# First tile and first weights asked for by two queues, and norm weights spread in eight single passes

## The chip, the cores and the metric

The kernel runs on one core of a Trainium2 chip. The metric is device time in microseconds of one execution; the median of several runs counts. Times inside the profile are microseconds from the start of the span.

## The reference

One layer of a gated streaming encoder on x of 1024 tokens by 1024 features, float32. Every row is normalised, projected once, and the columns of the projection feed two branches.

```python
h = rmsnorm(x, norm_g[l])
proj = h @ w_in[l]
q, k, v, za, u, vs, zs, gm = jnp.split(proj, IN_SPLITS, axis=-1)
a = window_sink_attention(rope(q), rope(k), v, att_sinks[l])
a = (a * jax.nn.silu(za)) @ w_att_out[l]
sgo = chunked_spatial_gating(gelu(u), gelu(vs), sg_w[l], sg_b[l], sg_ln_g[l], sg_ln_b[l])
sgo = (sgo * jax.nn.silu(zs)) @ w_sg_out[l]
ga, gs = jnp.split(jax.nn.sigmoid(gm + b_merge[l]), 2, axis=-1)
x = x + (ga * a + gs * sgo) @ w_o[l]
return rmsnorm(x, final_g)
```

with `rmsnorm(x, g) = x * rsqrt(mean(x*x) + EPS) * g`.

## The kernel before

Matrix products are made at float32 accuracy from single-pass fp32r operands: each operand is split into a high part, which is a cast to fp32r on ScalarE (ACT), and a low part, which is the difference, on VectorE (DVE) or GpSimd (POOL). A product is then three matmuls: high by high, high by low, low by high. Most of the kernel works in such products on two-by-two blocks with seven block products (`gemm_pair`); that part isn't touched by the diff.

The diff lies in the head, the first 20 us or so. The rows of x come in as eight tiles of 128 tokens (`load_x`), tile 0 as two halves of 512 columns. `scale_of` squares a tile and sums it on ACT, and `rstd_of` makes the reciprocal root: a square root on ACT (L145) and four small operations on DVE. `normed_tile` then, for each half of the columns, multiplies the tile by that root and by the norm weights on DVE (L625), transposes it in four 128x128 steps on TensorE (L632), casts the result to the high part on ACT (L635) and subtracts for the low part on DVE (L636).

The norm weights must lie on all 128 partitions for L625. They come in as two rows of 512 on partitions 0 and 32 of a zeroed tile `g_rows` (load at L563), and two fp32 matmuls with a selector `of_g` of ones and zeros spread them into the PSUM tiles `g_in` (L575). Matmuls on a tile of ones, whose result isn't used (`keep_busy`, L568), run ahead of the spread (six) and behind it (two), and `after` fixes this order.

The first columns of the big product are those of the spatial gate's input (`vs`). Its weights come in eight tiles of 512 KB; of the first four, numbers 0 and 1 go to `T_t3h`, 2 and 3 to `T_t4h` (`load_vs`, L655), number 0 in two halves. `split_vs` splits number 0 by halves, with its casts on ACT (L672) and its subtractions on POOL (L675), the others whole (L662 on ACT, L664 on DVE). `vs_gemm(0)` (L685) is the first product; the others are L646.

All of the head's loads are issued by SP, in the order tile 0 (two halves), norm weights, weights 0 (two halves), weights 1, row tile 1, weights 2, weights 3, row tile 2, row tile 3. A scheduler puts the instructions of each engine in order; each engine then works through its own list and waits on semaphores.

Of the kernel before, what the change touches and what calls it, by code (L numbers as in the profile page):

```python
# [25 lines left out]
F32 = mybir.dt.float32  # L26
F32R = mybir.dt.float32r
BF16 = mybir.dt.bfloat16
AF = mybir.ActivationFunctionType
# [3 lines left out]
P = 128  # L33
D = 1024
S = 1024
KC = D // P
HALF = 512
# [8 lines left out]
W_VS = 34  # L46
# [8 lines left out]
def hybrid_tile(  # L55
# [16 lines left out]
    nc = tc.nc  # L72
# [8 lines left out]
    def nm(s):  # L81
        count[0] += 1
        return f"{s}_{count[0]}"

    def bank(tag, dt=F32):
        return psum.tile([P, 512], dt, name=nm("ps_" + tag), tag="ps_" + tag, bufs=2)

    def mtile(shape, dt, tag, bufs, pool=None):
        return (pool or main).tile(shape, dt, name=nm(tag), tag=tag, bufs=bufs)
# [4 lines left out]
    def raw_tile():  # L94
        return mtile([P, D], F32, "wr", 3)
# [4 lines left out]

    eps_sb = const.tile([P, 1], F32, name="eps_sb")
    nc.gpsimd.memset(eps_sb[:], EPS)
    ones_b = mtile([P, HALF], BF16, "T_b22l", 1)
    nc.vector.memset(ones_b[:], 1.0)
    g_rows = mtile([P, D], F32, "wh", 3)[:, 0:HALF]
    nc.vector.memset(g_rows, 0.0)
    of_g = mtile([P, D], F32, "wl", 3)[:, 0 : 2 * P].rearrange("p (j m) -> p j m", j=2)
    nc.gpsimd.memset(of_g, 0.0)
    for j in range(2):
        nc.gpsimd.memset(of_g[32 * j : 32 * j + 32, j, :], 1.0)  # L110
    ident = const.tile([P, P], F32, name="ident")
    make_identity(nc, ident[:])
    warm = const.tile([P, 1], F32, name="warm")
    nc.scalar.activation(warm[:], eps_sb[:], AF.Sqrt)

    sink_sb = const.tile([P, 8], F32, name="sink_sb")
    nsink_sb = const.tile([P, 8], F32, name="nsink_sb")
# [59 lines left out]
    def after(second, first):  # L177

        tc.add_manual_dep(
            second.ins,  # L180
            first.ins.name,
            mybir.DependencyInfo(mybir.DependencyClass.NoSync, mybir.DependencyReason.DATA),
            reason="order",
        )
# [5 lines left out]
    def slot(name, shape=(P, 4, HALF), dt=F32R):  # L190

        return mtile(list(shape), dt, "T_" + name, 1)
# [362 lines left out]
    def load_x(t, parts=1):  # L555
        xt = raw_tile()
        for c in range(parts):
            cs = slice(c * D // parts, (c + 1) * D // parts)
            nc.sync.dma_start(xt[:, cs], x[t * P : (t + 1) * P, cs])
        return xt  # L560

    x_in = {0: load_x(0, 2)}
    nc.sync.dma_start(g_rows[0:33:32, :], norm_g.rearrange("(j n) -> j n", j=2))  # L563
    junk = mtile([P, D], F32, "wl", 3)

    def keep_busy(n):
        return [
            nc.tensor.matmul(idle[:], ones_b[:, 0:P], ones_b[:], start=True, stop=True) for _ in range(n)  # L568
        ]

    idle = bank("o")
    g_in = [bank("sc") for _ in range(2)]
    behind = keep_busy(6)[-1]
    for j in range(2):
        spread = nc.tensor.matmul(g_in[j][:], of_g[:, j, :], g_rows, start=True, stop=True)  # L575
        after(spread, behind)
        behind = spread
    after(keep_busy(2)[0], behind)

    hb = new_b(("b11", "b21"))  # L580

# [18 lines left out]
    def scale_of(t):  # L600
        xt = x_in[t] if t in x_in else load_x(t)
        if t == 0:
            s0, s1, base, half_base = (stat() for _ in range(4))
            for c, ss in enumerate((s0, s1)):
                nc.scalar.activation(junk[:, half_of(c)], xt[:, half_of(c)], AF.Square, accum_out=ss[:])
            nc.vector.tensor_scalar(base[:], s0[:], 1.0 / D, EPS, op0=ALU.mult, op1=ALU.add)
            nc.vector.tensor_scalar_mul(half_base[:], base[:], -0.5)
            return xt, rstd_of(s1[:], 1.0 / D, (base[:], half_base[:]))
        ss = stat()
        square = nc.scalar.activation(junk[:], xt[:], AF.Square, accum_out=ss[:])  # L610
        if t == 1:

            after(square, casts[-1])
        return xt, rstd_of(ss[:], 1.0 / D)

    def normed_tile(t, scale=None):
        xt, r = scale or scale_of(t)
        if t == 4:
            hb.update(new_b(("b22",)))
            f.update((n, slot(at, dt=F32)) for n, at in (("f12", "t4h"), ("f22", "t3h")))  # L620
        turned = []
        for j in range(2):
            cs = half_of(j)
            scalings.append(
                nc.vector.scalar_tensor_tensor(  # L625
                    xt[:, cs], xt[:, cs], r[:], g_in[j][:], op0=ALU.mult, op1=ALU.mult
                )
            )
            pt = bank("o" if t == 1 else "tp")
            for i in range(4):  # L630
                k = j * 4 + i
                nc.tensor.transpose(pt[:, i * P : (i + 1) * P], xt[:, k * P : (k + 1) * P], ident[:])  # L632
            p3 = pt[:].rearrange("p (k c) -> p k c", k=4)
            hi, lo = quarter_of(t, j)
            casts.append(nc.scalar.copy(hi, p3))  # L635
            los.append(nc.vector.tensor_sub(lo, p3, hi.bitcast(F32)))  # L636
            turned.append((f[f"f{j + 1}{t // 4 + 1}"][:, :, tokens(t)], p3))
            if t:
                nc.scalar.copy(*turned.pop())
        return turned  # L640
# [7 lines left out]

    vs_w, vs_casts = [], []

    def load_vs(c):
        parts = 2 if c == 0 else 1
        for i in range(parts):
            cs = slice(i * D // parts, (i + 1) * D // parts)
            nc.sync.dma_start(vs_raw[c // 2][:, c % 2, cs], w[W_VS + c][:, cs])  # L655

    def split_vs(c):

        raw = vs_raw[c // 2][:, c % 2, :].rearrange("p (k n) -> p k n", k=2)
        hi, lo = (v[c // 2][:, 2 * (c % 2) : 2 * (c % 2) + 2, :] for v in vs_split)  # L660
        if c:
            cast = nc.scalar.copy(hi, raw)  # L662
            vs_casts.append(cast)
            sub = nc.vector.tensor_sub(lo, raw, hi.bitcast(F32))  # L664
            if c == 1:
                after(sub, los[1])
            elif c == 2:
                after(cast, roots[1])
                after(sub, scalings[3])
        else:  # L670
            for k in range(2):
                cast = nc.scalar.copy(hi[:, k, :], raw[:, k, :])  # L672
                if k == 0:
                    after(cast, roots[0])
                nc.gpsimd.tensor_tensor(lo[:, k, :], raw[:, k, :], hi[:, k, :].bitcast(F32), op=ALU.subtract)  # L675
        vs_w.extend((hi[:, k, :], lo[:, k, :]) for k in range(2))
# [11 lines left out]
        nc.scalar.copy(xh[:, t, 0:HALF], acc[:])  # L688

    unsplit = normed_tile(0)  # L690
    vs_raw = [slot(n, (P, 2, D), F32) for n in ("t3h", "t4h")]
    vs_split = [[slot(n + e) for n in ("t1", "t2")] for e in "hl"]
    load_vs(0)
    load_vs(1)
    split_vs(0)
    x_in[1] = load_x(1)
    split_vs(1)
    second = scale_of(1)
    for c in (2, 3):
        load_vs(c)  # L700
    x_in[2] = load_x(2)
    normed_tile(1, second)
    for c in (2, 3):
        split_vs(c)
# [71 lines left out]
    for c in range(4):  # L776
        if c + 2 < 4:
            weights.append(vs_weights(c + 2))
        for t in range(NT):
            wh, wl = weights[c]  # L780
# [696 lines left out]
    with tc.manual_schedule(engines={mybir.EngineType.PE, mybir.EngineType.Activation, mybir.EngineType.DVE}):  # L1477
        p = 0
# [292 lines left out]
    for p in range(4):  # L1771
        n, t, acc, x11 = N_PAIRS + p, T_ORDER[p], accs[p], firsts[p]
# [203 lines left out]
```

## Time and profile before

| | us |
|---|---|
| median of 3 runs | 921.29 |
| lowest and highest run | 920.75, 921.34 |
| the profiled execution | 921.45 |
| its span | 919.7 |
| TensorE busy | 907.4 |
| ACT busy | 529.6 |
| DVE busy | 691.2 |

In a row of the timeline the first number is the start, the second the time that the row's instructions took together, then engine, line, operation, output and inputs, how many there were, and in brackets how long the engine had been idle before and what ended that. SPq and ACTq are the queues' DMA issues. In the chain of waits a row is start, length, and what held the end up then. In the table of windows the columns are the stretch and its length, busy time of TensorE, its weight loads, DVE, ACT and POOL with the number of instructions, the granted clock, the share of DMA time and GB/s.

### The profile page before, as it was taken

The numbers are of one execution on the slowest core, as the hardware profiler recorded it, in microseconds if no ns is written. First come the engines' busy times: TensorE is split into PE (matmuls) and PEld (weight loads), VectorE is DVE, ScalarE is ACT, GpSimd is POOL, SyncE is SP. The second block draws the span as 40 slices with busy tenths as digits, with TensorE's granted clock in tenths as the row PEclk, the third lists the DMA queues.
The fourth block names the chain that finished last, engine by engine and source line by source line (L and its number), as shares of the span: only waits on it lengthen the run. The fifth ranks groups of instructions, "written<-read, shape, count | busy, mean of one in ns | idle before, by whom it ended". The sixth has DMA issues, their size and how long they took to land.

```text
span 919.7 us, 13199 instructions
## 1 busy us (share of the span) xinstructions
PE 907.4 (99%) x4296; PEld 749.4 (81%) x4296; DVE 691.2 (75%) x1233; ACT 529.6 (58%) x1058; POOL 141.9 (15%) x213
## 2 busy tenths in 40 slices
PE   8999999999999999999999999999999999999996
PEld 5888888888888888888888888888888888887885
DVE  6774776656678678777887788765599689579986
ACT  7942433334445456877778878444476475467443
POOL 1002222213011001222111110001110111210012
PEclk9999999999999999999999999999999999999999
DMA  7328788877788879999999994775568666998633
GB/s 241 122 97 217 172 150 185 177 186 212 242 270 260 270 249 328 266 241 260 255 344 246 266 246 144 284 252 179 173 204 304 226 206 179 282 322 271 206 115 114
DMA packets 129024, 206.10 MB, mean 224 GB/s; under 512 B 12634, under 2 KB 59738, under 8 KB 128956
## 3 DMA queue, kind: packets, MB, share of 16 engines
q1 hardware_dynamic: 107292, 146.27, 49.3%
q0 software_dynamic: 21376, 58.73, 27.2%
q8 instruction: 34, 0.56, 0.3%
q14 instruction: 34, 0.28, 0.1%
q10 hardware_dynamic: 288, 0.26, 0.1%
HBM read 148.46 MB, written 90.31 MB: 260 GB/s over the span
## 4 chain that ended last, share of the span: by engine, by line
PE 88%; DVE 4%; ACT 3%; DMA 3%; issue 1%; SPq 0%; ACTq 0%
PE ps_mm L388 40%; PE ps_o L388 24%; PE ps_mm L646 6%; PE ps_tp L388 4%; PE ps_sc L1196 2%; PE ps_o L1320 2%; PE ps_sc L388 2%; PE ps_tp L857 2%; PE ps_tp L646 1%; PE ps_sc L646 1%; PE ps_o L646 1%; PE ps_tp L1267 1%; ACT pr L1231 1%; PE ps_tp L1272 1%; ACT pr L1254 1%
## 5 line engine op out<-in xcount | busy, mean ns | idle before, releaser
L174 ACT CAST wh<-s 128x1024 fp32r<-128x1024 f32 (+1 forms) x78 | 77.9, 1002 | 78.9 <-PE ps_mm L388 25.4
L175 DVE TENSOR_TENSOR wl<-s,wh 128x1024 fp32r<-128x1024 f32 (+1 forms) x78 | 90.9, 1166 | 21.6 <-ACT wh L174 21.4
L175 DVE TENSOR_TENSOR wl<-wr,wh 128x1024 fp32r<-128x1024 f32 (+1 forms) x64 | 60.3, 944 | 53.0 <-ACT wh L174 53.0
L174 ACT CAST wh<-wr 128x1024 fp32r<-128x1024 f32 (+1 forms) x64 | 53.0, 829 | 77.2 <-PE ps_mm L388 33.7
L1231 ACT ACTIVATE pr<-ps_sc,sm 128x192 f32<-128x192 f32 (+2 forms) x128 | 51.2, 407 | 30.6 <-DVE sm L1222 22.0
L333 POOL DMA_DIRECT2D sums<-in_w_dram x48 | 36.6, 861 | 207.4 <-PE ps_mm L388 86.4
L388 PE MATMUL ps_o<-T_b22h,wh 128*128 128x512 f32 x148 | 59.3, 401 | 0.0
L388 PE MATMUL ps_o<-T_t1h,wl 128*128 128x512 f32 x148 | 58.0, 392 | 0.4 <-DVE wl L175 0.4
L388 PE MATMUL ps_o<-T_t1h,wh 128*128 128x512 f32 x148 | 58.3, 394 | 0.0
L388 PE MATMUL ps_o<-T_b22l,wh 128*128 128x512 f32 x148 | 57.8, 390 | 0.0
L388 PE MATMUL ps_o<-T_b22h,wl 128*128 128x512 f32 x148 | 57.7, 390 | 0.0
L388 PE MATMUL ps_o<-T_t1l,wh 128*128 128x512 f32 x148 | 57.7, 390 | 0.0
L388 PE MATMUL ps_mm<-T_t4h,wh 128*128 128x512 f32 (+1 forms) x144 | 55.8, 388 | 0.0
L388 PE MATMUL ps_mm<-T_t2h,wh 128*128 128x512 f32 x140 | 55.5, 396 | 0.0
L388 PE MATMUL ps_mm<-T_t4l,wh 128*128 128x512 f32 (+1 forms) x144 | 55.3, 384 | 0.0
L388 PE MATMUL ps_mm<-T_t4h,wl 128*128 128x512 f32 (+1 forms) x144 | 55.3, 384 | 0.0
L388 PE MATMUL ps_mm<-T_b11h,wh 128*128 128x512 f32 x140 | 55.2, 394 | 0.0
L388 PE MATMUL ps_mm<-T_t3h,wh 128*128 128x512 f32 x140 | 54.8, 391 | 0.0
L388 PE MATMUL ps_mm<-T_b11l,wh 128*128 128x512 f32 x140 | 54.7, 391 | 0.0
L388 PE MATMUL ps_mm<-T_b11h,wl 128*128 128x512 f32 x140 | 54.6, 390 | 0.0
L388 PE MATMUL ps_mm<-T_t3h,wl 128*128 128x512 f32 x140 | 54.6, 390 | 0.0
L388 PE MATMUL ps_mm<-T_t2h,wl 128*128 128x512 f32 x140 | 54.5, 390 | 0.0
(405 smaller groups left out, 2470.2 us busy)
## 6 DMA issues: line engine op xcount, KB each, us to landing
wr<-in_w_dram SPq DMA_DIRECT2D x80, 256.0 KB
sums<-in_w_dram POOLq DMA_DIRECT2D x24, 512.0 KB, 6.7
s<-sums SPq DMA_DIRECT2D x24, 512.0 KB
wr<-in_w_dram SPq DMA_DIRECT2D x16, 512.0 KB
q_hl<-qhl SPq DMA_DIRECT2D x16, 512.0 KB
q<-q_hl SPq DMA_DIRECT2D x64, 128.0 KB
y_dr<-x POOLq DMA_DIRECT2D x28, 256.0 KB, 6.5
sums<-in_w_dram POOLq DMA_DIRECT2D x24, 256.0 KB, 7.4
```

What stands on the lines that cost most here:

```text
L174: nc.scalar.copy(hi, src)
L175: return nc.vector.tensor_sub(lo, src, hi.bitcast(F32))
L333: return lambda: paced(nc.gpsimd.dma_start(dst, src, accum_op=op))
L388: mm = nc.tensor.matmul(acc, lt, rt, start=fresh and k == 0 and n == 0, stop=k == 3 and n == 2, skip_group_check=True,)
L646: mm = nc.tensor.matmul(acc, lt, rt, start=k == 0 and n == 0, stop=k == KC - 1 and n == 2)
L857: nc.tensor.matmul(pm[:, t * P : (t + 1) * P], xh[:, half * 4 + t, g * P : (g + 1) * P], bias[-1][1][:, g % 4, :], start=True, stop=True,)
L1196: nc.tensor.matmul(sc[:, i, lo:hi], q_of[:, c, i * P : (i + 1) * P], kt[:, f, lo:hi], start=f == 0, stop=f == 1,)
L1231: nc.scalar.activation(st.pr[:, i, place_of(c, lo, hi)], st.sc[c][:, i, lo:hi], AF.Exp, bias=st.nmax[:, c, i : i + 1], scale=-1.0, accum_o ...
L1254: nc.scalar.mul(v, v, st.inv[:, c, i : i + 1])
L1267: nc.tensor.transpose(st.inner[0:wide, at : at + P], st.pr[:, i, place_of(c, 64 if st.t else P, 192)], ident[:])
L1272: nc.tensor.transpose(st.ends[0:wide, i * P : (i + 1) * P], st.pr[:, i, P : P + wide], ident[:])
L1320: nc.tensor.matmul(st.po[:, cs], lt, rt, start=i == 0, stop=i == len(terms) - 1, skip_group_check=True)
```

## The change

The second half of row tile 0 and the second half of weights 0 are issued by ACT's queue instead of SP's, ahead of ACT's table load, and the loads of weights 0 are issued right behind the norm weights. The norm weights come in as four rows of 256 on partitions 0, 32, 64 and 96. DVE casts them to a high part and subtracts for a low part, and eight fp32r matmuls of 256 columns (four rows by two parts) take the place of the two fp32 matmuls of 512. The selector has four blocks instead of two and is cast on DVE. Four keep-busy matmuls follow the spread instead of two. The splitting of weights 3 gets the same two order constraints as that of weights 2.

In the resulting order of instructions ACT casts the second half of weights 0 ahead of the square root of tile 0, where it was behind it, and casts weights 3 ahead of a copy of tile 0's transposes; SP issues the load of row tile 4 behind four small loads and that of `sg_w` instead of ahead of them. Everything else keeps its order on every engine.

```diff
+    g_rows = mtile([P, D], F32, "wh", 3)[:, 0:256]
+    nc.vector.memset(g_rows, 0.0)
     ones_b = mtile([P, HALF], BF16, "T_b22l", 1)
     nc.vector.memset(ones_b[:], 1.0)
-    g_rows = mtile([P, D], F32, "wh", 3)[:, 0:HALF]
-    nc.vector.memset(g_rows, 0.0)
-    of_g = mtile([P, D], F32, "wl", 3)[:, 0 : 2 * P].rearrange("p (j m) -> p j m", j=2)
-    nc.gpsimd.memset(of_g, 0.0)
-    for j in range(2):
-        nc.gpsimd.memset(of_g[32 * j : 32 * j + 32, j, :], 1.0)
+    rows_of = mtile([P, D], F32, "wl", 3)[:, 0:HALF]
+    nc.gpsimd.memset(rows_of, 0.0)
+    for j in range(4):
+        nc.gpsimd.memset(rows_of[32 * j : 32 * j + 32, j * P : (j + 1) * P], 1.0)
+    of_g = mtile([P, D], F32R, "wl", 3)[:, 0:HALF]
+    nc.vector.tensor_copy(of_g, rows_of)
+    g_split = mtile([P, D], F32R, "wh", 3)
+    g_parts = [g_split[:, i * 256 : (i + 1) * 256] for i in range(2)]
...
-    nc.scalar.activation(warm[:], eps_sb[:], AF.Sqrt)
...
-            nc.sync.dma_start(xt[:, cs], x[t * P : (t + 1) * P, cs])
+            (nc.scalar if c else nc.sync).dma_start(xt[:, cs], x[t * P : (t + 1) * P, cs])
         return xt
 
+    def load_vs(c):
+        parts = 2 if c == 0 else 1
+        for i in range(parts):
+            cs = slice(i * D // parts, (i + 1) * D // parts)
+            (nc.scalar if i else nc.sync).dma_start(vs_raw[c // 2][:, c % 2, cs], w[W_VS + c][:, cs])
+
     x_in = {0: load_x(0, 2)}
-    nc.sync.dma_start(g_rows[0:33:32, :], norm_g.rearrange("(j n) -> j n", j=2))
+    nc.sync.dma_start(g_rows[0:97:32, :], norm_g.rearrange("(j n) -> j n", j=4))
+    vs_raw = [slot(n, (P, 2, D), F32) for n in ("t3h", "t4h")]
+    load_vs(0)
+    nc.scalar.activation(warm[:], eps_sb[:], AF.Sqrt)
+    nc.vector.tensor_copy(g_parts[0], g_rows)
+    nc.vector.tensor_sub(g_parts[1], g_rows, g_parts[0].bitcast(F32))
...
     behind = keep_busy(6)[-1]
-    for j in range(2):
-        spread = nc.tensor.matmul(g_in[j][:], of_g[:, j, :], g_rows, start=True, stop=True)
-        after(spread, behind)
-        behind = spread
-    after(keep_busy(2)[0], behind)
+    for j in range(4):
+        for i in range(2):
+            spread = nc.tensor.matmul(
+                g_in[j // 2][:, j % 2 * 256 : j % 2 * 256 + 256],
+                of_g[:, j * P : (j + 1) * P],
+                g_parts[i],
+                start=i == 0,
+                stop=i == 1,
+            )
+            after(spread, behind)
+            behind = spread
+    after(keep_busy(4)[0], behind)
...
             if c == 1:
                 after(sub, los[1])
-            elif c == 2:
+            else:
                 after(cast, roots[1])
                 after(sub, scalings[3])
...
-    load_vs(0)
     load_vs(1)
```

More of the change, by code (lines that the diff above doesn't have):

```diff
@@ L649, in hybrid_tile @@
     vs_w, vs_casts = [], []
[L651 to L655, printed above, removed]
     def split_vs(c):
@@ L690, in hybrid_tile @@
     unsplit = normed_tile(0)
-    vs_raw = [slot(n, (P, 2, D), F32) for n in ("t3h", "t4h")]
     vs_split = [[slot(n + e) for n in ("t1", "t2")] for e in "hl"]
-    load_vs(0)
     load_vs(1)
```

## The prediction

> **What bounds the kernel now.** I read the page first: TensorE is busy in 99% of the span. So only the time before its steady run can move, and I read the chain that ended last for the first 30 us, then the timeline of that stretch, for who holds it up.
>
> ```profile
> PE 907.4 (99%) x4296; PEld 749.4 (81%) x4296; DVE 691.2 (75%) x1233; ACT 529.6 (58%) x1058; POOL 141.9 (15%) x213
> ...
> 2.70 0.34 SPq L655
> 3.04 0.04 issue
> ...
> 3.58 6.02 DMA T_t3h<-in_w_dram
> ...
> 9.62 1.05 ACT T_t1h L662
> 10.66 0.49 ACT T_b11h L635
> ...
> 16.45 4.81 PE ps_mm L646 x20
> ```
>
> The chain starts with issues on SP, goes through one transfer (the second weight tile, 512 KB into T_t3h, asked for at 3.58, landed at 9.60), then its cast on ACT, and only then the cast of tile 0's transposes, which sits behind it in ACT's queue. From 16.4 TensorE runs on, 20 matmuls in 4.81 us, 0.24 each. Whatever the change gives must appear as an earlier 16.41.
>
> The timeline shows ACT full from that landing up to the cast that releases TensorE:
>
> ```profile
> 9.62 1.05 ACT L662 CAST T_t1h<-T_t3h 128x1024 fp32r<-128x1024 f32 x1 [2.04 <-DMA T_t3h<-in_w_dram]
> 10.57 0.58 ACT L635 CAST T_b11h<-ps_tp 128x512 fp32r<-128x512 f32 x1
> 11.04 0.59 ACT L635 CAST T_b21h<-ps_tp 128x512 fp32r<-128x512 f32 x1
> 11.52 1.07 ACT L610 ACTIVATE wl<-wr 128x1024 f32<-128x1024 f32 x1
> ...
> 14.27 1.41 DVE L625 SCALAR_TENSOR_TENSOR wr<-wr,st,ps_sc 128x512 f32<-128x512 f32 x2
> 14.33 1.05 ACT L662 CAST T_t2h<-T_t4h 128x1024 fp32r<-128x1024 f32 x1
> 15.77 0.58 ACT L635 CAST T_b11h<-ps_o 128x512 fp32r<-128x512 f32 x1
> 16.41 0.50 PE L646 MATMUL ps_mm<-T_t1h,T_b11h 128*128 128x512 f32 x1
> ```
>
> On ACT no row after the first names a wait, and the rows between touch. So 16.41 is the landing at 9.60 plus 6.8 us of fixed work, and the spread of norm weights, which the diff rewrites most visibly, is not on this path as long as tile 0's transposes are ready when ACT asks for them.
>
> **The landing of the second weight tile.**
>
> ```profile
> 0.74 0.86 SPq L559 DMA_DIRECT2D wr<-in_x_dram  x2
> 0.91 0.48 DVE L104 MEMSET T_b22l<- 128x512 bf16 x1 [0.91 <-PEq L1964]
> 1.16 0.45 POOL L110 MEMSET wl<- 32x128 f32 x2
> 1.46 0.48 DVE L106 MEMSET wh<- 128x512 f32 x1
> 1.97 0.69 SPq L563 DMA_DIRECT2D wh<-in_norm_g_dram  x1
> 5.91 0.62 ACT L672 CAST T_t1h<-T_t3h 128x512 fp32r<-128x512 f32 x1 [0.74 <-DMA T_t3h<-in_w_dram]
> 6.96 0.62 ACT L672 CAST T_t1h<-T_t3h 128x512 fp32r<-128x512 f32 x1 [0.43 <-DMA T_t3h<-in_w_dram]
> 3.00:3.50 0.50, 0.50 (x2) 0.15 (x1) 0.00 (x0) 0.10 (x1) 0.00 (x0) 1.00 0.82 315
> 3.50:4.00 0.50, 0.50 (x2) 0.00 (x0) 0.00 (x0) 0.50 (x2) 0.00 (x0) 1.00 0.38 90
> 4.00:4.50 0.50, 0.20 (x1) 0.00 (x0) 0.31 (x2) 0.50 (x3) 0.00 (x0) 1.00 0.95 221
> ```
>
> SP spends 0.43 on each half of tile 0, then waits for the memset that ends at 1.94, spends 0.69 on the norm weights, and asks for the first weight half only at 2.70. The last two columns of the windows are the share of DMA time and GB/s: the engines fall from 315 to 90 GB/s between 3.5 and 4.0, because nothing more has been asked for in time.
>
> The change moves tile 0's second half and the first weight tile's second half to ACT's queue, and puts a memset half as wide ahead of the bf16 one. That memset ends between 0.91 + 0.24 = 1.15 (proportional to columns) and 1.39 (no shorter). So SP asks for the norm weights at 1.17 to 1.41, for the first weight half 0.69 + 0.04 later, at 1.90 to 2.14, and for the second weight tile 0.34 + 0.04 later, at 2.28 to 2.52: 1.06 to 1.30 earlier. But its bytes queue behind the 1 MB of tile 0 and the first weight tile on the same engines. If the engines are the limit, only the hole is won: filled at the mean of its neighbours, (315 + 221)/2 = 268, it holds (268 - 90) x 0.5 = 89 KB, or 0.33 us at 268. If asking is the limit, 1.06 to 1.30 are won. The hole's share of 0.38 speaks for asking; so do the cast rows, by which the first tile's halves land 1.05 us apart (5.89 and 6.94), 256 KB at 250 GB/s with engines that had moved 315. The 6.02 us from asking to landing speak for the engines. I take 1.0, close to the issue's end, because the nearest rows show engines that wait for work. Bounds 0.3 and 1.3. No row shows two queues disturbing each other; it would cost the same sort of fraction, and I let the gain fall to zero in the range.
>
> The Trainium skill, in "Trainium Kernel Development and Optimization", Key Constraints, speaks against hoping for more: transfers asked for by SP and ACT run on the same 16 engines and interleave, and several askers save only the sequencer's issue time. By that rule the sum ends at the 1.30 of earlier issue, 920.15, and rival (2) below falls; this trace has no two queues at work together to set against it.
>
> **What ACT pays for two issues.**
>
> ```profile
> L1826 ACTq DMA_DIRECT2D out_dram<-g x2: 375/407/439, 915.6 to 916.0; - x2
> 0.73 1.28 ACT L114 ACT_TABLE_LOAD   x1 [0.73 <-PEq L1964]
> 3.40 0.63 ACT L605 ACTIVATE wl<-wr 128x512 f32<-128x512 f32 x1 [1.17 <-DMA wr<-in_x_dram]
> 4.12 0.63 ACT L605 ACTIVATE wl<-wr 128x512 f32<-128x512 f32 x1
> ```
>
> Two issues of 0.41 stand ahead of the table load, which moves by 0.82. The 1.17 us that ACT waits for tile 0 hide it: no cost, unless the issues take over 0.58 each. Tile 0's halves now share the engines, so the first square starts between 3.40 and 4.12 and the pair ends at 4.85 to 5.57.
>
> **Tile 0's own path, the cover.** Three things meet before its transposes: the root, the spread, the keep-busy matmuls.
>
> ```profile
> 4.88 0.29 ACT L145 ACTIVATE st<-st,st 128x1 f32<-128x1 f32 x1
> 5.66 0.21 DVE L152 TENSOR_SCALAR st<-st,st 128x1 f32<-128x1 f32 x1
> 4.88 3.75 PE L575 MATMUL ps_sc<-wh,wl 128*128 128x512 f32 x4 [0.68 <-DMA wh<-in_norm_g_dram]
> 8.67 0.75 DVE L625 SCALAR_TENSOR_TENSOR wr<-wr,st,ps_sc 128x512 f32<-128x512 f32 x1 [0.96 <-PE ps_sc L575]
> 8.42 1.02 PE L568 MATMUL ps_o<-T_b22l 128*128 128x512 bf16 x2
> 9.28 1.04 PE L632 MATMUL ps_tp<-ident,wr 128*128 128x128 f32 x8
> 11.20:14.73 3.53, 3.52 (x13) 2.28 (x13) 3.42 (x8) 3.50 (x7) 0.00 (x0) 1.00 0.93 371
> 909.45 0.28 PE L388 MATMUL ps_mm<-T_t4h,wh 128*128 128x256 f32 x1
> ...
> 912.20 0.28 PE L388 MATMUL ps_mm<-T_t4h,wl 128*128 128x256 f32 x1
> L958 DVE COPY rot<-rot 128x128 f32<-128x128 f32 x8 | 1.3, 220 | 3.1 <-DMA rot<-in_sin_dram 1.8 <-DMA rot<-in_cos_dram 1.3
> L976 DVE SCALAR_TENSOR_TENSOR qhl<-x,qhl 128x256 fp32r<-128x256 f32 x32 | 12.0, 421 | 3.3 <-ACT qhl L974 3.3
> ```
>
> Root: in the new ACT order the cast of the first weight tile's second half stands ahead of the square root, a new wait. That half lands at 6.94 now and is asked for 1.9 earlier: landing 5.0 to 6.9, and I take 5.9, the same 1.0 as above. Cast 0.62, root 0.29, then 0.70 on DVE as now (5.17 to 5.87): 7.55. The scalings of 0.75, the second starting 0.70 behind the first (two run in 1.41 later on), end at 8.3 and 9.0, against 9.42 now.
>
> Spread: the norm weights land at 4.85 now, and are asked for 0.56 to 0.80 earlier: 4.1 to 4.85. High part by a copy (0.22 at 128 columns, 0.42 for two sources at 256: some 0.3), low part 0.42; TensorE's last input is there at 4.8 to 5.6. The 24 single passes of 256 columns at the end start 2.75/23 = 0.12 apart at full clock. Here the clock is at half: the two bf16 matmuls ahead of the transposes stand (9.28 - 8.42)/2 = 0.43 apart, against 0.24 later. So 0.24 a pass; the upper end is the old fp32 pass, 3.75/4 = 0.94 for 512 columns with the last one's tail, 0.47 for 256. Eight passes: 1.9, at most 3.8, where four fp32 passes took 3.75. Four keep-busy matmuls add 4 x 0.43 = 1.7, where two took 0.86. With the likely values: 5.0 + 1.9 + 1.7 = 8.6 for the first transposes, 0.6 for four: 9.2. The second four follow the scaling at 9.0: 9.8 at most.
>
> ACT asks for them at 8.6 + 1.05 = 9.65 and 10.1. So tile 0's path is covered by 0.45 and 0.3 us and costs nothing; uncovered (all upper ends: 5.6 + 3.8 + 1.7 + 0.6 = 11.7 against 10.57 now) it would cost 1.1.
>
> Answered in one go: POOL's selector, done at 1.61 now, gets two more memsets of 0.22 and one that is twice as wide; even 0.8 more for that and 0.6 for the copy on DVE end at 3.5, ahead of the norm weights. The bf16 memset is now second, so the six keep-busy matmuls start some 0.25 later and end inside the 0.68 that TensorE is idle now. Casting the fourth weight tile ahead of a PSUM copy keeps ACT's sum. On SP the load of row tile 4 stands behind four small loads and the 512 KB of sg_w, which are free to go while SP waited for a buffer.
>
> **Sum.** Span 919.7 less 1.0; the profiled execution's 921.45, with its 1.75 outside the span, becomes 920.45. The median of the runs is 0.16 below that execution: **920.3**.
>
> **Rivals.** (1) *Hidden transfer*: engines limit the landing, 0.3 won: 921.0. For it: those 6.02 us. Against it: the hole. (2) *More than the issue*: two queues also close the gaps between the halves, the tile lands at 7.5 to 8.0, and root and spread take their early ends. The root's path then has the first transposes done at 5.0 + 0.62 + 0.29 + 0.70 + 0.75 + 0.6 = 8.0, the spread's at 4.8 + 1.9 + 1.7 + 0.6 = 9.0, or 8.5 with passes 0.18 apart; against 10.57 now 1.6 to 2.1 are won: 919.2 to 919.7. Against it: spread and keep-busy hold the transposes until 8 whatever the transfers do. (3) *The half clock stays*, slower: now TensorE's unbroken run is 4.88 to 9.28, 4.4 us; it becomes about 4.9 to 8.6, 3.7 us. If the full clock isn't granted by about 10, where tile 0's products start (11.20 less 1.0), the 13 matmuls ahead of tile 1's transposes and those eight take 13 x 0.43 + 1.04 = 6.6: tile 1 is turned at 16.8, where it is at 16.41 now, and at 17.9 if the transposes double. That is 0.4 to 1.5 slower, and (0.43 - 0.24)/0.43 = 0.44 more for each us that the clock stays half behind that, 1.3 for three: 921.7 to 924.1. Against it: keep-busy ahead of the spread runs on almost without a gap now. The Trainium skill, "TensorE: Matmul & The Clock Gate", Part 1, gives a free-running window of some 3.4 us that must be busy for the full clock; by its figure the shorter run leaves that window less slack, and the trace's first full-rate matmuls, behind 9.28, don't contradict it.
>
> **Chances.** Forecast 0.50, (1) 0.16, (2) 0.22, (3) 0.12. A measurement of this kernel tells about 0.2% (1.84 us) from no change, so faster begins at 919.45 and slower at 923.13. Of (2), which straddles the first bound, I count 0.14 beyond it, and 0.08 of the forecast for what the landing may give that no row shows: faster 0.22. Of (3) 0.08 lie beyond the second: slower 0.08. The rest is 0.70. The range goes from (2)'s end, 919.2, past a gain of zero into (3), 922.0.
>
> **What would show it.** Right: the second weight tile's cast on ACT starts near 8.6 with a DMA as releaser, TensorE's unbroken run starts near 15.4, spread passes 0.24 apart, and everything behind is unchanged. Wrong: a cast of tile 0's transposes that waits for TensorE, matmuls 0.43 apart behind 11, or a landing after 9.3.

## The result, and the profile after

| | median us (lowest to highest, runs) | ratio to before, 95% interval |
|---|---|---|
| before | 920.75 (919.01 to 922.13, 17) | |
| the change | 922.4 (921.08 to 924.36, 17) | 1.002 [1.0012, 1.0027] |
| the change, measured again with the experiments (before there 921.36) | 921.94 (920.56 to 923.4, 11) | 1.0004 [0.9995, 1.0013] |

The change makes the kernel 1.65 us slower; forecast was 920.3, at most 922.0. In the second measurement the two can't be told apart, so the size of the loss isn't fixed, but a gain of 1.0, as forecast, is excluded in both. The profiled execution took 922.64, its span 920.9, against 921.45 and 919.7.

The chain of waits after (start, length, what held the end up):

```profile
1.19 3.72 DMA wh<-in_norm_g_dram
...
5.36 2.32 PE ps_sc L590 x8
7.68 1.73 PE ps_o L582 x4
9.41 0.87 PE ps_tp L653 x4
10.28 0.02 issue
10.30 0.59 ACT T_b11h L656
...
15.56 0.64 PE ps_o L653 x4
16.20 0.02 SPq L562
16.23 0.04 issue
16.27 8.03 DMA wr<-in_x_dram
24.30 0.02 issue
24.32 1.15 ACT wl L631 x2
```

Two things are new. The head no longer hangs on the second weight tile but on the norm weights, their spread (L590), the keep-busy matmuls (L582) and tile 0's transposes. And where TensorE ran on unbroken from 16.4, a transfer of 8.03 us stands in the chain: row tile 4, asked for at 16.27, landed at 24.30.

The timeline after: the rows of ACT that wait for the weight tile, for TensorE and for row tile 4; TensorE's spread and transposes; and SP's issues.

```profile
7.46 1.05 ACT L677 CAST T_t1h<-T_t3h 128x1024 fp32r<-128x1024 f32 x1 [0.65 <-DMA T_t3h<-in_w_dram]
10.30 0.59 ACT L656 CAST T_b11h<-ps_tp 128x512 fp32r<-128x512 f32 x1 [1.79 <-PE ps_tp L653]
...
24.32 1.06 ACT L631 ACTIVATE wl<-wr 128x1024 f32<-128x1024 f32 x1 [2.18 <-DMA wr<-in_x_dram]
...
5.36 2.32 PE L590 MATMUL ps_sc<-wh,wl 128*128 128x256 f32 x8 [0.89 <-DVE wh L576]
...
9.20 1.65 PE L653 MATMUL ps_tp<-ident,wr 128*128 128x128 f32 x8
...
11.25 1.35 SPq L806 DMA_DIRECT2D sink_sb<-in_sinks_dram  x2
12.65 0.60 SPq L809 DMA_DIRECT2D bm_sb<-in_b_merge_dram  x1
13.29 0.43 SPq L810 DMA_DIRECT2D lg_sb<-in_ln_g_dram  x1
13.77 0.43 SPq L811 DMA_DIRECT2D lb_sb<-in_ln_b_dram  x1
14.24 0.43 SPq L828 DMA_DIRECT2D wT<-in_sg_w_dram  x1
16.27 0.33 SPq L562 DMA_DIRECT2D wr<-in_x_dram  x1
```

The weight tile lands at 7.44, 2.2 us earlier than at 9.60, but ACT then waits 1.79 for TensorE, so all but 0.2 of it is lost again (TensorE's run starts at 16.24 instead of 16.41). Later ACT waits 2.18 for row tile 4, whose load is the last of these SP rows. In the kernel before, the first rows of SP from the sinks on, and ACT's row for row tile 4, are:

```profile
10.72 1.36 SPq L793 DMA_DIRECT2D sink_sb<-in_sinks_dram  x2
16.53 0.34 SPq L559 DMA_DIRECT2D wr<-in_x_dram  x1
16.91 0.43 SPq L796 DMA_DIRECT2D bm_sb<-in_b_merge_dram  x1
...
22.22 1.06 ACT L610 ACTIVATE wl<-wr 128x1024 f32<-128x1024 f32 x1
```

There only the sinks are ahead of row tile 4, bm, lg, lb and sg_w follow it, and ACT's row names no wait. So three small loads and sg_w changed places with it, not four and sg_w: the sinks stand ahead of it in both kernels. The table of windows says what the transfers do meanwhile (TensorE busy first; last two columns DMA share and GB/s; the clock's column reads 1.00 also ahead of the first grant on record, and so says nothing of the head), before and then after:

```profile
5.50:11.00 5.50, 4.82 (x14) 2.01 (x12) 1.83 (x4) 2.62 (x4) 2.65 (x3) 1.00 0.91 331
...
16.00:18.50 2.50, 2.50 (x13) 1.88 (x12) 2.50 (x4) 2.50 (x6) 0.00 (x0) 1.00 0.42 109
18.50:21.00 2.50, 2.50 (x13) 2.06 (x12) 2.39 (x8) 1.88 (x5) 0.00 (x0) 1.00 0.93 261
...
23.50:26.00 2.50, 2.50 (x14) 1.83 (x13) 2.31 (x6) 2.13 (x6) 0.00 (x0) 1.00 0.50 195
```

```profile
5.50:11.00 5.50, 5.41 (x21) 3.89 (x21) 2.78 (x10) 3.06 (x8) 2.65 (x3) 1.00 1.03 417
...
16.00:18.50 2.50, 2.45 (x12) 1.87 (x11) 2.50 (x4) 2.39 (x6) 0.00 (x0) 1.00 0.44 105
18.50:21.00 2.50, 2.50 (x13) 2.02 (x12) 2.39 (x8) 2.08 (x5) 0.00 (x0) 1.00 0.68 194
21.00:23.50 2.50, 2.50 (x17) 2.09 (x15) 1.95 (x7) 0.81 (x3) 0.00 (x0) 1.00 0.61 221
23.50:26.00 2.50, 0.31 (x3) 0.01 (x1) 0.68 (x2) 1.68 (x4) 0.00 (x0) 1.00 0.58 214
```

TensorE loses 2.19 of the 2.50 us behind 23.5. The DMA engines aren't full when row tile 4 is due: 194 and 221 GB/s (18.5 to 23.5), where the loads of the head ran at 417. Something slow seems to stand in the queue. From 26 us on the instructions of DVE start 2.0 us later than before, and after some 340 us, where other waits take part of it in, 1.1 to 1.6: a gain of 0.2, a loss of 2.2, and 0.8 of it given back.

### The profile page after: what moved, and what is told of

Read it like the earlier page. It is cut to its first block, busy times and chain, and to the rows that moved or that the text cites. A ratio compares the mean times of both kernels' runs of the same rounds, so it can differ in the third digit from the quotient of the medians.

```text
span 920.9 us, 13215 instructions
## 1 busy us (share of the span) xinstructions
PE 907.0 (98%) x4302; PEld 751.0 (82%) x4302; DVE 692.9 (75%) x1236; ACT 529.7 (58%) x1058; POOL 142.8 (16%) x215
## 4 chain that ended last, share of the span: by engine, by line
PE 83%; DVE 7%; ACT 6%; DMA 2%; issue 2%; ACTq 0%; SPq 0%; DVEq 0%
PE ps_mm L391 37%; PE ps_o L391 24%; PE ps_mm L667 5%; PE ps_tp L391 4%; PE ps_sc L391 2%; ACT pr L1244 2%; PE ps_tp L870 2%; PE ps_sc L1209 2%; DVE sm L1234 1%; PE ps_o L1333 1%; DVE pTb L1316 1%; PE ps_tp L667 1%; PE ps_sc L667 1%; PE ps_o L667 1%; DVE aT L1347 1%
```

## The experiments

Each ran in five rounds beside the kernel before on the same chip, whose medians were 920.9, 920.97, 921.0, 921.36 and 921.39 in the five groups.

**Group 1: put row tile 4 ahead of the small loads.** The first theory was the order alone; rivals were the clock, which by the trace's own record is granted in full from 10.45 instead of 9.27, and the keep-busy matmuls. `a_x4_first` puts all six loads behind row tile 4, the sinks too, which the kernel before has ahead of it:

```diff
-    nc.sync.dma_start(bm_sb[:], b_merge)
+    after(nc.sync.dma_start(bm_sb[:], b_merge), x_loads[4])
```

and the same for the sinks, lg, lb, sg_w and sg_b.

> The changed kernel with one thing put back: SP issues the load of row tile 4 ahead of the sinks, the three other small loads, sg_w and sg_b, as the kernel before does. Theory 1, queue order: the load, asked for at 16.3, landed at 24.30 in the changed kernel because it stood behind thousands of packets of 8 to 64 bytes; now it lands by 20, TensorE's wait of 2.2 us at tile 4 is gone, and the time falls from 922.4 by 1.5 to 2.2 to 920.2 to 920.9, level with the kernel before or 0.5 below it. Theory 2, half clock: what costs is the clock, granted at 10.4 where it was 9.3; this edit doesn't touch it, and the time stays at 922.4.

`b_x4_late` is the kernel before with the sinks, bm, lg and lb ahead of row tile 4 (sg_w behind it):

> The kernel before with one thing changed: SP issues the sinks and the three other small loads (not sg_w) ahead of row tile 4's load. Theory 1, queue order: tile 4's load lands after 22 where it landed by 19.75, TensorE waits some 2 us for it, and the time rises from 920.75 by 1.2 to 2.2. Theory 2, half clock: no part of the clock's history changes ahead of 16.4, so 920.75.

`a_one_queue` is `a_x4_first` with all loads back on SP (`nc.scalar if c else nc.sync` becomes `nc.sync`), so that of the change the second queue is gone and the new spread stays:

> The changed kernel with row tile 4's load first, and all loads of the head on SP's queue again, so that only the new spread is left of the change. Theory 1, queue order: the second weight tile lands near 9.3 (the norm weights are still asked for earlier), TensorE's steady run starts at 16.1 to 16.4, and the time is that of the kernel before, 920.5 to 920.9. Theory 2, half clock: spread and keep-busy are those of the changed kernel, so its loss stays, 922 to 922.4.

`a_x4_first_kb2` is `a_x4_first` with `keep_busy(2)` behind the spread instead of `keep_busy(4)`:

> Row tile 4's load first, and two keep-busy matmuls behind the spread instead of four. Theory 3, keep-busy is the gate: in the changed kernel the second weight tile landed 2.15 us earlier, but tile 0's transposes waited until 9.20 for the spread and 4 x 0.43 of keep-busy, so the steady run began only 0.17 earlier. With two it begins 0.86 earlier, near 15.4, and the time is 0.6 to 0.9 below that of the run with four. Theory 2, half clock: the shorter run keeps the clock at half for longer, the transposes and tile 0's products run at 0.43 apart, and the time is 0.4 to 1.5 above that of the run with four.

| | median us | ratio |
|---|---|---|
| a_x4_first | 924.19 | 1.0034 [1.0021, 1.0048] |
| b_x4_late | 920.6 | 0.9998 [0.9988, 1.0008] |
| a_one_queue | 923.45 | 1.0035 [1.0024, 1.0046] |
| a_x4_first_kb2 | 923.82 | 1.0035 [1.0022, 1.0048] |

The first theory missed three of three. The chains of `a_x4_first`, `a_one_queue` and `a_x4_first_kb2` show why:

```profile
22.83 8.15 DMA wr<-in_x_dram
```

```profile
22.24 7.99 DMA wr<-in_x_dram
```

```profile
21.32 8.54 DMA wr<-in_x_dram
```

Row tile 4 now comes in time, and row tile 5 takes its place behind the small loads: 8 us again, for which ACT waits 3.08, 2.92 and 3.47 us. So my repair had only moved the wait. `b_x4_late` has no such row. Two of these stalls cost a second time: behind them the clock falls back to half for 3.41 us (`a_x4_first` from 34.44, `a_x4_first_kb2` from 33.32; not in `a_one_queue`). TensorE's run starts at 15.34 with two keep-busy matmuls and at 16.84 with four, but the norm weights landed 0.86 later in the profile with four (5.77 against 4.91), so at most some 0.6 is left for the matmuls; the medians differ by 0.4, which is within their noise.

**Group 2: behind all row tiles, and by halves.** `x_loads[4]` becomes `x_loads[7]`: for all six loads (`a_all_x_first`, and `a_all_x_kb2` with two keep-busy matmuls), for the small loads only (`a_small_late`), for sg_w and sg_b only (`a_wt_late`).

> The changed kernel, with the sinks, bm, lg, lb, sg_w and sg_b asked for only behind row tile 7's load, so that no row tile stands behind them. Theory 4 (the loss is a row tile's load queued behind the small-packet loads and sg_w; in the changed kernel tile 4's, in the earlier experiments tile 5's): the casts of row tiles wait for no DMA, TensorE's run starts at 16.2 and goes on unbroken, 920.4 to 920.9 beside a kernel before of 920.8. Rival (the later full clock, 10.45 instead of 9.27, is the loss): the time stays at that of the changed kernel, 922.0 to 922.6, although no row tile is waited for. Third possibility (the small loads cost wherever they stand): a new wait of 1 to 3 us shows behind row tile 7, at the next weights, 921.5 to 923.

> As the kernel with all row tiles first, and with two keep-busy matmuls behind the spread instead of four. Theory 4 with the keep-busy matmuls as the gate of the first transposes: the run starts at 15.3 as it did with tile 4 first and two of them, now no row tile stalls it, so 0.9 below the kernel with four: 919.5 to 920.0. Half-clock rival: two fewer keep TensorE less busy, the full clock comes no earlier, nothing is won against four: 922.

> The changed kernel with only the sinks, bm, lg and lb behind row tile 7; the 512 KB of sg_w and sg_b stay where they are, ahead of tile 4. If the 896 small packets are what holds tile 4: its wait is gone (sg_w alone is 1.3 to 2 us of transfer, asked for 2 us ahead of tile 4), 920.4 to 921.0. If the bytes of sg_w are: tile 4 is waited for by 1.5 to 2.2 us as in the changed kernel, 922.0 to 922.6. Half-clock rival: 922.0 to 922.6 without a wait.

> The changed kernel with only sg_w and sg_b behind row tile 7; the sinks, bm, lg and lb stay ahead of tile 4. If the small packets hold tile 4: the wait stays at 1.0 to 2.2 us, 921.6 to 922.6. If the bytes of sg_w do: no wait, 920.4 to 921.0. Half-clock rival: 922.0 to 922.6 without a wait.

| | median us | ratio |
|---|---|---|
| a_all_x_first | 920.45 | 0.9994 [0.9985, 1.0003] |
| a_all_x_kb2 | 919.91 | 0.9987 [0.9979, 0.9996] |
| a_small_late | 920.69 | 0.9998 [0.9989, 1.0007] |
| a_wt_late | 920.18 | 0.9987 [0.9978, 0.9995] |

In none of them does ACT wait for a row tile behind tile 0, and the loss is gone. (In `a_all_x_first` ACT waits 2.0 us for the weights behind row tile 7, which TensorE doesn't feel.) The rival of the later full clock falls: `a_small_late` was granted it at 11.0, later than the change, and is level with before. `a_small_late` and `a_wt_late` each take only one half away, and each suffices: small packets alone or sg_w alone are not enough for the wait, both ahead of the row tile are. By my expectations one of the two should have kept the wait; that was wrong.

**Group 3: the order of before.** `a_old_order` lets the sinks go as they do and puts bm, lg, lb, sg_w and sg_b behind `x_loads[4]`, so that SP's list is that of before and every other engine's that of the change. `a_old_order_kb2` has two keep-busy matmuls, `a_old_kb2_one_queue` all loads on SP besides. `b_both_ahead` puts the order of the change into the kernel before.

> The changed kernel with SP's queue put back in the order of before: the sinks ahead of row tile 4, and bm, lg, lb, sg_w and sg_b behind it; the order on all other engines is that of the changed kernel. Theory 4 (row tile 4's load behind small packets and sg_w is the loss): no cast of a row tile waits for a DMA, the run starts at 16.2, 920.2 to 920.9 beside a kernel before of 920.9. Rival (moving loads far back, behind row tile 7, had won something else): only part of the 1.65 us comes back, 921.3 to 922.4.

> The same with two keep-busy matmuls behind the spread instead of four: the run starts at 15.5, 0.7 earlier, and nothing stalls: 919.5 to 920.2. If the pause behind row tile 7 that follows an early start (row tiles and weights late) eats it: as with four, 920.2 to 920.9.

> The same with two keep-busy matmuls, and tile 0's and the first weight tile's second halves asked for on SP again. If asking on two queues is what the change can win: the second weight tile lands at 8.9 as with one queue earlier, its cast is the gate again, the run starts 6.83 behind it, at 15.8 against 15.5: 0.2 to 0.3 more than with two queues. If tile 0's path (norm weights, spread) is the gate in both: no difference.

> The kernel before with only row tile 4's load put behind bm, lg, lb and sg_w on SP, the order of the changed kernel; first tile, weights, spread and keep-busy as before. Theory 4: row tile 4 is waited for by 1 to 2.5 us and the kernel is 1 to 2 us slower than before: 921.9 to 922.9. Rival (the order costs only together with the new head): no wait, 920.8. The order of some later instructions on ACT, DVE and TensorE moves with it, since the order of the queues is planned together.

| | median us | ratio |
|---|---|---|
| a_old_order | 920.46 | 0.9993 [0.9984, 1.0001] |
| a_old_order_kb2 | 919.64 | 0.9986 [0.9977, 0.9995] |
| a_old_kb2_one_queue | 920.76 | 0.9997 [0.9988, 1.0006] |
| b_both_ahead | 921.17 | 1.0003 [0.9994, 1.0012] |

With bm, lg, lb and sg_w put back behind row tile 4 (sg_b was behind it already), no row tile is waited for, and the change is no slower than before. This is the loss, shown by one edit: TensorE runs the same list of instructions as in the change. The interval lies below that of the change's first measurement and overlaps with that of the second. Two queues are then worth 1.1 us (919.64 against 920.76): in the chains of these two, TensorE's run starts at 15.63 and at 16.66.

```profile
8.53 1.72 PE ps_tp L655 x8
...
15.63 4.86 PE ps_mm L669 x20
```

```profile
3.29 6.51 DMA T_t3h<-in_w_dram
...
16.66 4.82 PE ps_mm L669 x20
```

But `b_both_ahead` shows no wait, against the theory that the order alone decides. It isn't a clean test, because the lists are planned together: its sinks were asked for at 8.82, 2.4 us ahead of the change's 11.25 (though their packets moved no earlier, from 13.78 to 18.63), and ACT takes row tile 4 only at 24.32, where the kernel before takes it at 22.22. By the trace's packets its load was through by 21.5. Still, a second condition was missing.

**Group 4: why the small loads are slow.** The trace's packets, counted by size and start, show the sinks: 512 packets of 8 bytes, which read the same 64 bytes 64 times over.

```
kernel            packets of 8 bytes   first start   last start
before            512                  13.86         17.50
the change        512                  13.30         21.25
a_wt_late         512                  13.43         18.51
a_old_order       512                  13.34         18.17
```

A packet takes 0.008 us on its engine, and there are 16 engines, so 512 could pass in 0.3 us. They take 3.6 to 8. With no large load moving (`a_wt_late`, 14 to 17 us) they pass at 52 to 54 in each half us, one in 9.4 ns, as if in single file; in the change, once sg_w's packets are between them, mostly at half of that or less. `a_sinks_early` asks for the sinks ahead of row tile 2, `a_sinks_other` lets the same packets read other addresses, so that the sinks' values are left out of the computation:

```diff
-            ... of_head[e].partition_broadcast(64)
+            ... other[e * 64 : (e + 1) * 64, :, 0:2]
```

with `other = w[W_VS].rearrange("p (c q) -> p c q", c=4)`. `a_old_order_kb0` has no keep-busy matmul behind the spread; `changed_again` is the change.

> The changed kernel unaltered, on the chip of the next three: 922.0 to 922.8 beside a kernel before of 920.9, row tile 4 waited for by some 2 us in the profile.

> The changed kernel with the sinks asked for ahead of row tile 2's load, while 2 MB of weights and rows are in flight; bm, lg, lb and sg_w stay ahead of tile 4, and the order on all other engines is that of the changed kernel. If the packets are slow because they are asked for behind loads that have already landed: they pass within 3 us behind the loads in flight, tile 4 is waited for by less than 0.5 us, 920.3 to 921.0. If what counts is only that sg_w and small packets stand ahead of tile 4: bm, lg and lb are only 384 packets and sg_w 512 KB, a wait of 0.3 to 1.0 us stays, 920.8 to 921.6. If the sinks are slow wherever they stand: they take 4 to 8 us, row tiles 2 and 3 behind them land late, and the first stall comes at tile 2 or 3: 922 or more.

> The changed kernel with the sinks' two loads reading 512 pairs of numbers at other addresses, 1 KB apart, out of a weight, instead of the same 64 bytes 64 times over; so the sinks' values are left out of the computation. Number, size and order of the packets stay. If the same address is the cost: the 512 packets pass within 1 us, as 384 packets of bm, lg and lb do in the kernel before, tile 4 isn't waited for, 920.3 to 921.0. If the count of packets is the cost: they still take 4 us or more, tile 4 is waited for by some 2 us, 922.0 to 922.8.

> The changed kernel with SP's order of before and no keep-busy matmul behind the spread. Transposes start behind the spread at 7.7; then the weight tile's cast on ACT (8.1, done 9.2) is the gate, and the run starts at 15.0 to 15.3: 919.2 to 919.7, 0.3 below the one with two. If the full clock needs the keep-busy matmuls: granted later than 11, the run starts at 16 or later, 920.5 or more.

| | median us | ratio | 8-byte packets |
|---|---|---|---|
| changed_again | 921.94 | 1.0004 [0.9995, 1.0013] | 12.89 to 20.30 |
| a_sinks_early | 921.04 | 1.0001 [0.9993, 1.001] | 9.98 to 15.61 |
| a_sinks_other | 920.01 | 0.9986 [0.9977, 0.9995] | 13.58 to 15.01 |
| a_old_order_kb0 | 920.08 | 0.9991 [0.9982, 1.0001] | 11.73 to 16.55 |

`a_sinks_other` decides it. Number, size and order of the packets are those of the change, and they pass in 1.4 us instead of 7.4 to 8; ACT waits for no row tile, and the windows show engines that move again (compare the change's 0.44 and 105). ACT's row for row tile 4, and the window:

```profile
21.97 1.06 ACT L631 ACTIVATE wl<-wr 128x1024 f32<-128x1024 f32 x1
...
16.00:18.50 2.50, 2.45 (x11) 1.95 (x11) 2.50 (x4) 2.29 (x6) 0.00 (x0) 1.00 0.85 274
```

The Trainium skill, "DMA: Bandwidth & Descriptors", Why small descriptors are slow, gives a fixed cost for each packet and its descriptor; by that the change and `a_sinks_other` would be alike, and the measurement says that here it is the place that is read. Whether it must be the same bytes, or neighbours would do, wasn't tried. `a_sinks_early` shows that the slow packets go along: they still take 5.6 us, and now row tile 2, the next behind them, is late by 1.40 us, which TensorE hardly feels (it is busy 9.58 of the 10 us behind 16):

```profile
17.30 1.06 ACT L633 ACTIVATE wl<-wr 128x1024 f32<-128x1024 f32 x1 [1.40 <-DMA wr<-in_x_dram]
```

`changed_again` has the same chain as the change (row tile 4: asked for at 15.84, landed 7.49 later, 1.70 of ACT's time), with a smaller loss. My hope of 0.3 more from `a_old_order_kb0` failed: its median is 0.4 above the one with two (919.64, in group 3). In its profile the full clock is granted only at 13.9, and TensorE's run starts at 16.35, but that execution, 922.77, is the longest of its eleven.

**Group 5: the same sinks in whole rows.** SP's order is that of the change; the sinks come as one row of 64 bytes for each partition, and two copies on DVE much later pick the halves.

```diff
-    for e in range(2):
-        nc.sync.dma_start(
-            sink_sb[...].rearrange("p (c r) -> p c r", r=2), of_head[e].partition_broadcast(64)
-        )
+    nc.sync.dma_start(sink_all[:], sinks.partition_broadcast(P))
```

> The changed kernel, SP's order unchanged, but the sinks loaded as one row of 64 bytes for each of 128 partitions instead of 512 pieces of 8 bytes; two small copies later on DVE pick each half. If each packet that reads the same place costs about 9.4 ns in turn (512 in 4.8 us elsewhere): 128 take 1.2 us, row tile 4 isn't waited for, 920.0 to 920.7 beside a kernel before of 920.9. If reading the same place is slow by bytes (128 x 64 bytes is twice the bytes): 5 us or more, tile 4 is waited for by 1 to 2 us, 921.5 to 922.5.

> The same with two keep-busy matmuls behind the spread: the run starts at 15.5, no tile is waited for, 919.4 to 920.0, as with SP's order of before and two keep-busy matmuls. If tile 4 is waited for: the early start is lost in that wait, 921.5 to 922.5.

| | median us | ratio |
|---|---|---|
| a_sinks_whole | 920.13 | 0.9988 [0.9979, 0.9996] |
| a_sinks_whole_kb2 | 919.68 | 0.9982 [0.9974, 0.9991] |

All packets of 64 bytes (these 128 and bm's 128) pass between 13.20 and 14.65, and no row tile is waited for, although bm, lg, lb and sg_w stay ahead of row tile 4. So the cost goes by packets that read one place, not by their bytes, of which there are twice as many as in the change. `a_sinks_whole_kb2` beats the kernel before by 1.7 us, and the interval of its ratio lies below those of the change in both measurements. Its chain has no transfer behind the norm weights':

```profile
1.18 3.66 DMA wh<-in_norm_g_dram
...
8.49 0.85 PE ps_tp L654 x4
...
15.26 4.80 PE ps_mm L668 x20
20.06 0.44 PE ps_tp L654 x4
```

## Why the prediction was wrong

**The landing of the second weight tile.** The direction was right, the size wrong: forecast 1.0 earlier with bounds 0.3 and 1.3, measured 2.2 (7.44 against 9.60; 7.57 in the second profile). The asking came as forecast, 1.2 earlier (2.37 against 3.58). The rest wasn't in the sum: the half tile ahead of it was asked for by ACT at 1.18, 1.9 earlier than 3.09, and the windows from 5.5 to 11 went from 331 to 417 GB/s. The bound that I took from the Trainium skill ("Trainium Kernel Development and Optimization", Key Constraints), that several askers save only issue time, I had worked out from this tile's own issue alone, 1.30. (Its 920.15 there is the time of the profiled execution; as a median it would be 920.0.) With the loads back on SP the tile landed at 8.9 and 9.8 (`a_one_queue`, `a_old_kb2_one_queue`), with two queues at 7.0 to 8.7 over the profiles. Rival (2) had this part.

**ACT's two issues** cost nothing, as forecast: ACT still waits for tile 0, 1.11 us.

**Tile 0's path, the cover.** I called it covered by 0.45 and 0.3 us; it is the gate. First transposes were forecast at 8.6 and started at 9.41. The terms: norm weights landed at 4.91, just past the upper end of 4.85; the spread took 2.32, not 1.9, since a pass takes 0.29 at half clock, not 0.24; keep-busy 1.73 as forecast; four transposes 0.87 instead of 0.6, because the full clock came 1.2 later. With the tile landed 2.2 earlier instead of 1.0, ACT had nothing left but to wait, which is the first sign that I had named as wrong. Of a forecast gain of 1.0, 0.2 was left; two keep-busy matmuls instead of four bring back 0.4 to 0.8 us in the medians of the four pairs (0.82 with SP's order of before), all of one sign, though none by itself is clear of the noise.

**Row tile 4 on SP.** This is the step that made a loss of a small gain. The prediction said that four small loads (in fact three changed sides) and sg_w "are free to go while SP waited for a buffer" and gave them nothing. SP's issues were indeed free; row tile 4 was asked for at 16.27, even earlier than 16.53. What I left out is that the transfers in front of it have to be done: 896 small packets, 512 of them nearly in single file, and 512 KB. So the term that I put at nothing came to 2.18 us of waiting (1.70 in the second profile). The trace of before had it to be read: the sinks stand alone ahead of row tile 4, asked for at 10.72, and in 16.0 to 18.5, while they pass, the engines move 109 GB/s at a share of 0.42. I took a queue for free because its issuer was.

**The rivals.** All three lay in the head ahead of 16.4; none was the cause. (3), the half clock, has the right sign, but the full clock came at 10.45 and the run's start wasn't late; the change measured again was granted it at 9.28, as the kernel before at 9.27, and waits for row tile 4 all the same; and `a_all_x_first` to `a_wt_late` put the loss elsewhere. Whether the full clock needs the matmuls behind the spread isn't shown: the one profile without them has it at 13.93, the others between 5.2 and 11.1.

**The size of the loss** differs between the measurements, 1.65 and 0.6, and here the clock does come in, by another way than (3). In the first, seven of the change's 17 runs had a mean granted clock of 0.996 or less, with a median of 923.95; the other ten have 921.66. In the second none of 11 had, with a median of 921.94, which is 0.98 above those runs of the kernel before beside it whose clock was higher (920.96). The first ten are 0.98 above the same kind of runs of the kernel before, over all five groups (920.68). So without the low clock the change loses some 1.0 us in both measurements; the wait is in both profiles, 2.18 and 1.70. The two profiled executions with a clock of 0.996 or less (`a_x4_first`, `b_both_ahead`) each have a stretch of 3.41 us in which the clock fell back to half (`a_x4_first_kb2` has one at 0.997); where it lay in the seven runs no profile shows. The kernel before has such runs too, 47 of 152 over the five groups (median 921.71), and the nine kernels with two queues, keep-busy matmuls and no row tile waited for have none in 101. So a part of their gain over the kernel before is the clock: of the 1.7 of `a_sinks_whole_kb2`, 1.0 is left against the higher-clock runs beside it (920.67).

**Open** stays why sg_w's packets behind the sinks stretch them from 5 to 8 us, and why the runs of the kernel before lose the clock more often. That the order of the change costs only with slow sinks is shown; that it would cost in the kernel before with sinks asked for as late as 11.25 wasn't tried.

## What to carry to other kernels

When a scheduler lets a load slip behind others in a queue, price the transfers in front of it, not the time that the issuer spends on them, and ask when the buffer's user needs it. Look for loads that read one small place many times over: fetch whole rows and pick on an engine. And when a repair only moves the wait to the next tile, look at what stands in the queue before moving it once more.

## What was not expected of the hardware

512 packets of 8 bytes took 3.6 to 8.1 us when all read the same 64 bytes, and 1.4 us when they read 512 other places; one passed in 9.4 ns in the steady part, although its own record lasts 8 ns and there are 16 engines. 128 packets of 64 bytes of that same place passed, together with bm's 128, within 1.5 and 1.8 us (`a_sinks_whole`, `a_sinks_whole_kb2`).

The full clock was granted between 5.2 and 13.9 us over the profiled executions. In the 17 in which it then held, it lasts 904.53 or 907.95 us, 3.41 apart. In three it fell back to half for 3.41 us: in `b_both_ahead` in the middle of the head, in `a_x4_first` and `a_x4_first_kb2` right behind the stall at row tile 5. The seventh figure of these rows of windows is the granted clock, first of `b_both_ahead`:

```profile
13.50:16.00 2.50, 2.50 (x8) 1.83 (x7) 2.39 (x6) 2.13 (x4) 0.00 (x0) 0.52 0.50 154
```

Then of `a_x4_first`, where 10 matmuls ran in the 3.41 us, and 20 in the next 3.15:

```profile
34.44:37.85 3.41, 3.41 (x10) 2.64 (x9) 3.02 (x6) 3.23 (x6) 0.00 (x0) 0.50 0.40 154
37.85:41.00 3.15, 3.15 (x20) 2.63 (x19) 0.71 (x2) 2.55 (x4) 0.00 (x0) 1.00 0.01 3
```

This agrees with the Trainium skill, "TensorE: Matmul & The Clock Gate", Part 1, which gives a free-running window of some 3.4 us. Such a window more or less at half clock is part of the spread of single runs here.
